# Gate and up products of an expert in one branch or in two, by halves of the weights' rows

## The chip, the cores and the metric

The kernel runs on one core of a Trainium2 chip. The metric is the device time of one execution in microseconds, and the figure for a kernel is the median of its runs. Three runs of the kernel before took 1243.87, 1243.13 and 1238.35 us: the median is 1243.13 us, the mean 1241.78 us.

## The reference

The block has two halves. The first mixes tokens: a diagonal state-space mixer and a stick-breaking attention share an input projection and an output projection. The change does not touch it. The second is a routed mixture of experts over 1024 tokens of width 1024. Each token goes to two of 32 experts, and of each expert is computed

```python
def expert_block(args):
    xb, e = args
    return (jax.nn.silu(xb @ w_gate[e]) * (xb @ w_up[e])) @ w_down[e]
```

`w_gate` and `w_up` are 1024 by 512, `w_down` is 512 by 1024, all float32. So an expert has 6 MB of weights, and 32 of them 192 MB. The result is scaled by the gate and added to the token's row.

## The kernel before, in words

**Stages.** In the profiled execution the projections, the mixer and the attention take the span up to some 584 us, the routing that up to some 600 us, and the loop over the experts the rest. All times below are from the span's start.

**Weights.** SyncE streams the weights as units of 1 MB in one fixed order (`load_units`, the issue is line 855). An expert has four units for the gate and up products, `hv[0]` to `hv[3]`: gate rows of the first half, up rows of the first half, gate and up rows of the second half. Two more units are for the down product. The units go into a ring of 17 tiles (named `rg`, `q_t`, `yT` and `rw` after what the memory held before), and the issue of a unit waits on SyncE until TensorE has done the last read of the tile's former content.

**Order of the experts.** Experts are sorted by count, and large and small ones alternate. For 18 of the 32 places in this order `two(e)` (line 1246) holds: such an expert may have more than 128 tokens, so that the code for a second block of up to 128 tokens is compiled for it. The places are 0, 1, 2, 4, 6, 8, 10, 12, 14, 16, 17, 18, 20, 22, 24, 26, 28 and 30. Blocks past the second are left to a loop at the end.

**Branches.** All counts are only known at run time, and every engine reads them into a register (`prep_n`, line 1283, for TensorE). `by_count` (lines 1361 to 1369) chooses among three forms: "all" over 64 tokens (32 matmuls of 128 by 512, line 1204), "half" over 32 (line 1210) and "quarter" (line 1216). `past` (lines 1371 to 1379) holds two nested Ifs: over 128 tokens (line 1375), and in it over 192 (line 1376). Where an If on TensorE is not taken, the other side has an instruction that puts the semaphore count where the taken side would have left it, and this instruction waits until all matmuls before it have ended. I call this a drain.

**One turn of the loop** for place e has on TensorE: the gate and up products of e (`in_`, line 1420), the transposes of the gathered rows of e+1 (`prep_x`, line 1381, at line 1194), the down products of e-1 (`down_`, lines 1222, 1228 and 1234), the index products of a later expert (`prep_p`, line 1295) and the transposes of e's hidden rows (`h_`, line 1463, at line 1240). GpSimd gathers rows (line 1184) and scatters results (line 1189). VectorE writes the one-hot matrices that `prep_p` multiplies: `OHa` for the first 128 tokens (two buffers), and `OHb` for the second block (one buffer, `OH2`, cleared by GpSimd at line 920).

**What the diff touches.** In `in_` the first block's products stand with `past` for the second block in one `by_count` (`in_many`), which is the whole of `in_` for every place but 0. Place 0 has its products in two `by_count` with the first index products (`between`) in the middle.

By the branches that left instructions in the profiled execution, the 18 places fall into three classes. Places 4, 8, 16 and 24 have a second block. Places 10, 12, 18, 20, 26 and 28 take "all" and have none. The other eight (0, 1, 2, 6, 14, 17, 22 and 30) take "half".

Of the kernel before, what the change touches and what calls it, by code (L numbers as in the profile page):

```python
# [10 lines left out]
BF = mybir.dt.bfloat16  # L11
# [9 lines left out]
NT = 8  # L21
P = 128
# [14 lines left out]
def block_kernel(ctx, tc, x, g_mix, w_in, lam_re, lam_im, log_dt, b_re, b_im, c_re, c_im, d_skip,  # L37
                 w_glu, b_glu, g_q, g_k, g_so, g_ao, w_out, g_ffn, w_rg, b_rg, w_re, b_rexp,
                 w_gate, w_up, w_down, out, dbg=None, stop=99):
    nc = tc.nc  # L40
# [717 lines left out]
    kp = ctx.enter_context(tc.tile_pool(name="kp", bufs=1, side="right", reuse_waits="tile"))  # L758
# [138 lines left out]
    slot2 = kp.tile([P, P], BF, name="slot2")  # L897
    ts(slot2, slot, float(P), None, op0=OP.add)

    slot2m = kp.tile([P, P], BF, name="slot2m")  # L900
# [15 lines left out]
    ts(sideq, sideq, 32.0, None, op0=OP.is_ge)  # L916
    tt(sided, side, sideq, op=OP.subtract)

    OH2 = kp.tile([P, NT, P], BF, name="OHb")
    nc.gpsimd.memset(OH2, 0.0)  # L920
    memb = late.tile([P, NT, NE], BF, name="memb")
    gts = late.tile([P, NT, NE], F32, name="gts")
    x2s = {}
# [202 lines left out]
    posb = kp.tile([P, NT, NE], BF, name="posb")  # L1126
# [27 lines left out]
    def one_hot(t_, pe, sl):  # L1154
        shp = [P, NT, P]
        tt(t_, sl.unsqueeze(1).to_broadcast(shp), pe.to_broadcast(shp), op=OP.is_equal)

    def ohs():
        return kp.tile([P, NT, P], BF, name="OHa", bufs=2)
# [19 lines left out]
    def pb(tag, bufs=2):  # L1179
        return ps.tile([P, 512], F32, tag=tag, bufs=bufs, name=tag)  # L1180
# [20 lines left out]
    def in_all(p, xt, hv, ks=range(8)):  # L1201
        for k_ in ks:
            for j in range(2):
                mm(p[j], xt[:, k_], hv[2 * (k_ // 4) + j][:, 512 * (k_ % 4):512 * (k_ % 4) + 512],  # L1204
                   start=k_ == 0, stop=k_ == 7)

    def in_half(pg, xt, hv, ks=range(8)):
        for k_ in ks:
            for r, j in ((LO, 0), (HI, 1)):
                mm(pg[r], xt[:, k_, LO], hv[2 * (k_ // 4) + j][:, 512 * (k_ % 4):512 * (k_ % 4) + 512],  # L1210
                   start=k_ == 0, stop=k_ == 7)

    def in_quarter(pg, xt, hv, ks=range(4)):
        for k_ in ks:
            for u in range(4):
                mm(pg[32 * u:32 * u + 32], xt[:, 4 * (u // 2) + k_, QU], hv[u][:, 512 * k_:512 * k_ + 512],
                   start=k_ == 0, stop=k_ == 3)
# [24 lines left out]
    def two(e):  # L1242

        if e < NF:
            return True
        b = int(f"{e:05b}"[::-1], 2)
        return (b - 1 - (b > 16) - (b > 8) + 1) * (P + 1) <= 2 * T

    def prep(e):

        if e >= NE:
            return
        d = EX.setdefault(e, {})
        ev = slice(e, e + 1)
        if e >= NF:
            ev = bass.ds(nc.values_load(evi[0:1, e:e + 1], engines=[ET.DVE], min_val=0, max_val=NE - 1), 1)
        sl = kp.tile([P, P], BF, name="sl")
        stt(sl, mid, some[:, e:e + 1], slotq, op0=OP.mult, op1=OP.add)
        stt(sl, top, many[:, e:e + 1], sl, op0=OP.mult, op1=OP.add)
        d["oh"] = ohs()  # L1260
        one_hot(d["oh"], posb[:, :, ev], sl)
        d["ax"] = aux[:, :, ev, :]
        if e >= NF:
            d["ax"] = kp.tile([P, NT, 1, 5], BF, name="ax", bufs=2)
            nc.vector.tensor_copy(d["ax"], aux[:, :, ev, :])
        d["ce"] = csi[0:1, e:e + 1]
        d["ng"] = nc.values_load(d["ce"], engines=[ET.Pool], min_val=0, max_val=T + HP)
        d["nv"] = nc.values_load(d["ce"], engines=[ET.DVE], min_val=0, max_val=T + HP)
        if not two(e):
            return  # L1270
        with tc.If(d["nv"] > P):
            with tc.If(d["nv"] <= P + HP) as few:
                one_hot(OH2, posb[:, :, ev], slot2m)
            with few.Else():
                one_hot(OH2, posb[:, :, ev], slot2)

    def prep_n(e):

# [8 lines left out]
    def prep_p(e):  # L1287

        if e >= NE:
            return  # L1290
        d = EX[e]
        d["pi"] = pb("y")[:, 0:16].rearrange("p (b n) -> p b n", b=2)
        for b_, oh in enumerate((d["oh"], OH2)[:2 if two(e) else 1]):
            for i in range(NT):
                mm(d["pi"][:, b_, 0:5], oh[:, i], d["ax"][:, i, 0], start=i == 0, stop=i == NT - 1)

# [64 lines left out]
    def by_count(n, all_, half, quarter):  # L1361

        with tc.If(n > HP) as many_:
            all_()
        with many_.Else():
            with tc.If(n > HP // 2) as some_:
                half()
            with some_.Else():
                quarter()

    def past(e, n, all_, half):

        if not two(e):
            return
        with tc.If(n > P):  # L1375
            with tc.If(n > P + HP) as many_:
                all_()
            with many_.Else():
                half()
# [36 lines left out]
    def next_raws(n):  # L1416
        raw_k[0] += n
        return [raws.pop(raw_k[0] - n + j) for j in range(n)]

    def in_(e, between=None):  # L1420

        d = EX[e]
        pg, pu = pb("acc"), pb("acc")
        pg2, pu2 = (pb("gx"), pb("gx")) if two(e) else (None, None)
        hv = next_raws(4)

        def in_many():
            in_all((pg, pu), d["xt"], hv)
            past(e, d["nt"], lambda: in_all((pg2, pu2), d["xt2"], hv), lambda: in_half(pg2, d["xt2"], hv))

        if e:
            by_count(d["nt"], in_many, lambda: in_half(pg, d["xt"], hv), lambda: in_quarter(pg, d["xt"], hv))
        else:
            for a in range(2):
                by_count(d["nt"], lambda: in_all((pg, pu), d["xt"], hv, range(4 * a, 4 * a + 4)),
                         lambda: in_half(pg, d["xt"], hv, range(4 * a, 4 * a + 4)),
                         lambda: in_quarter(pg, d["xt"], hv, range(2 * a, 2 * a + 2)))
                if a == 0:
                    between()
            d["turn2"]()  # L1440
            d["second"]()
            past(e, d["nt"], lambda: in_all((pg2, pu2), d["xt2"], hv), lambda: in_half(pg2, d["xt2"], hv))
        d["p"] = pg, pu, pg2, pu2

    def in_out(e):
# [126 lines left out]
    d = EX[0]  # L1572
# [8 lines left out]
    mo = ctx.enter_context(tc.tile_pool(name="mo", bufs=1, side="right", reuse_waits="tile"))  # L1581
    xga = [mo.tile([P, D], F32, name=f"xga{j}") for j in range(3)]
    xgb = mo.tile([P, D], F32, name="xgb")
    d["xg"] = xga[0]
    gather(xga[0], idx0, AL)
    for t_ in (xga[1], xga[2], xgb):
        nc.gpsimd.memset(t_, 0.0)
    tt(away, away, cnt.unsqueeze(1).to_broadcast(sh), op=OP.mult)
    tt(posb, own, away, op=OP.add)
# [4 lines left out]
    mo2 = ctx.enter_context(tc.tile_pool(name="mo2", bufs=1, side="right", reuse_waits="tile"))  # L1594
    prep_x(0)
    prep(0)
    prep_n(0)
    prep(1)
# [54 lines left out]
    with tc.For_i(0, nx, 1) as j:  # L1653
        ev = nc.values_load(xei[0:1, bass.ds(j, 1)], min_val=0, max_val=NE - 1)
# [20 lines left out]
        xt = mo.tile([P, 8, P], F32, name="xt2")  # L1675
# [9 lines left out]
        pg, pu = pb("acc"), pb("acc")  # L1685
# [39 lines left out]
```

## Time and profile before

| what | value |
|---|---|
| runs | 1243.87, 1243.13, 1238.35 us |
| profiled execution | 1238.39 us, of it span 1236.6 us |
| mean granted TensorE clock | 0.961 of full speed |
| TensorE busy (PE) | 1083.4 us, 88% |
| VectorE busy (DVE) | 632.3 us, 51% |
| ScalarE busy (ACT) | 342.9 us, 28% |
| GpSimd busy (POOL) | 261.7 us, 21% |
| moved by DMA | 267.87 MB, of it 232.29 MB on SyncE's queue |

PE is the matmul side of TensorE, PEld its weight loads; a name with a q behind it (PEq, PEldq, SPq) is an engine's sequencer, which reads the instructions and does the branches. The profiled execution is 1.8 us longer than its span, and 4.74 us (0.38%) shorter than the median of the runs.

### The profile page before, as it was taken

The numbers are of one execution on the slowest core, as the hardware profiler recorded it, in microseconds if no ns is written. First come the engines' busy times: TensorE is split into PE (matmuls) and PEld (weight loads), VectorE is DVE, ScalarE is ACT, GpSimd is POOL, SyncE is SP. The second block draws the span as 40 slices with busy tenths as digits, with TensorE's granted clock in tenths as the row PEclk, the third lists the DMA queues.
The fourth block names the chain that finished last, engine by engine and source line by source line (L and its number), as shares of the span: only waits on it lengthen the run. The fifth ranks groups of instructions, "written<-read, shape, count | busy, mean of one in ns | idle before, by whom it ended". The sixth has DMA issues, their size and how long they took to land. (4 is left out here: it accounts for less than half of the span.)

```text
span 1236.6 us, 19598 instructions
## 1 busy us (share of the span) xinstructions
PE 1083.4 (88%) x6562; PEld 698.4 (56%) x6562; DVE 632.3 (51%) x1487; ACT 342.9 (28%) x656; POOL 261.7 (21%) x401
## 2 busy tenths in 40 slices
PE   5999999978999879998586897998899988999985
PEld 5999899976776647887232333444334433434432
DVE  6888777779788865666722323213241422321211
ACT  6225244366668564322100000001010010100011
POOL 4043122033334410222111112002020020211111
PEclk9999999998999999999697998999999999999998
DMA  7251322120001135436699599679999899999993
GB/s 252 86 105 38 56 68 67 35 85 18 2 1 24 52 130 194 147 125 239 252 380 370 197 364 371 234 277 352 387 382 397 316 309 377 366 406 382 358 392 71
DMA packets 95577, 267.87 MB, mean 217 GB/s; under 512 B 44308, under 2 KB 57432, under 8 KB 70840
## 3 DMA queue, kind: packets, MB, share of 16 engines
q1 hardware_dynamic: 80664, 232.29, 50.6%
q0 software_dynamic: 11232, 27.04, 8.8%
q10 hardware_dynamic: 3520, 6.46, 1.4%
q8 instruction: 93, 1.52, 0.5%
q14 instruction: 68, 0.56, 0.1%
HBM read 240.73 MB, written 23.86 MB: 214 GB/s over the span
## 5 line engine op out<-in xcount | busy, mean ns | idle before, releaser
L91 PE MATMUL acc<-wh,hTh 128*128 128x256 f32 x512 | 147.0, 287 | 4.4 <-ACT wh L87 4.4
L92 PE MATMUL acc<-wl,hTh 128*128 128x256 f32 x512 | 145.8, 285 | 0.0
L93 PE MATMUL acc<-wh,hTl 128*128 128x256 f32 x512 | 144.9, 283 | 0.0
L91 PEld LDWEIGHTS acc<-wh,hTh 128*128 128x128 f32 x512 | 97.5, 191 | 5.0 <-ACT wh L87 5.0
L1189 POOL DMA_INDIRECT out_dram<-ysa,idx x24 | 36.8, 1533 | 299.6 <-DVE idx L1304 112.8
L92 PEld LDWEIGHTS acc<-wl,hTh 128*128 128x128 f32 x512 | 97.6, 191 | 0.7 <-DVE wl L88 0.6
L93 PEld LDWEIGHTS acc<-wh,hTl 128*128 128x128 f32 x512 | 97.4, 190 | 0.0
L697 DVE TENSOR_TENSOR_SCAN bb<-bb,sb 128x128 f32<-128x128 f32 (+7 forms) x64 | 90.0, 1420 | 14.0 <-POOL bb L694 13.5
L694 POOL TENSOR_SCALAR bb<-sb 128x128 f32<-128x128 f32 (+7 forms) x64 | 64.7, 1015 | 96.1 <-ACT sb L693 84.3
L1457 DVE TENSOR_TENSOR hs<-hs,acc 128x512 f32<-128x512 f32 x10 | 6.9, 688 | 146.4 <-ACT hs L1453 83.6
L1194 PE MATMUL tr<-ident,xga 128*128 128x128 f32 x256 | 39.8, 303 | 34.7 <-DMA xga<-h2d,idx 26.9
L1194 PEld LDWEIGHTS tr<-ident,xga 128*128 128x128 f32 x256 | 33.3, 195 | 60.4 <-issue 34.8
L1204 PE MATMUL acc<-rw,xt 128*128 128x512 f32 x128 | 56.9, 592 | 0.0
L1189 POOL DMA_INDIRECT out_dram<-ysf,idx x12 | 18.9, 1574 | 175.7 <-ACTq L1375 77.4
L708 PE MATMUL tr<-ident,bb 128*128 128x128 f32 x288 | 45.8, 283 | 8.8 <-DVE aT L714 3.6
L1452 ACT ACTIVATE hs<-acc 128x512 f32<-128x512 f32 x10 | 6.0, 598 | 170.0 <-PEq L1375 78.4
L91 PE MATMUL acc<-wh,mh 128*128 128x512 f32 x128 | 52.2, 410 | 0.0
L721 PE MATMUL acc<-aT,v_t 128*64 128x128 f32 x576 | 46.2, 281 | 5.8 <-DVE aT L714 4.8
L93 PE MATMUL acc<-wh,ml 128*128 128x512 f32 x128 | 50.8, 397 | 0.0
L92 PE MATMUL acc<-wl,mh 128*128 128x512 f32 x128 | 50.6, 396 | 0.0
L1184 POOL DMA_INDIRECT xga<-h2d,idx x32 | 35.0, 1095 | 68.1 <-PE y L1234 19.2
L1210 PE MATMUL acc<-rw,xt 128*64 128x512 f32 x192 | 46.8, 603 | 1.8 <-issue 1.8
(510 smaller groups left out, 2334.8 us busy)
## 6 DMA issues: line engine op xcount, KB each, us to landing
rw<-in_w_down_dram SPq DMA_DIRECT2D x28, 1024.0 KB
rw<-in_w_gate_dram SPq DMA_DIRECT2D x28, 1024.0 KB
rw<-in_w_up_dram SPq DMA_DIRECT2D x27, 1024.0 KB
rg<-in_w_gate_dram SPq DMA_DIRECT2D x20, 1024.0 KB
rg<-in_w_up_dram SPq DMA_DIRECT2D x20, 1024.0 KB
rg<-in_w_down_dram SPq DMA_DIRECT2D x20, 1024.0 KB
wraw<-in_w_in_dram SPq DMA_DIRECT2D x16, 512.0 KB
yT<-in_w_up_dram SPq DMA_DIRECT2D x8, 1024.0 KB
```

Of the source, the lines that this page charges most:

```text
L91: mm(o, ah, bh, start=first, stop=False)
L92: mm(o, ah, bl, start=False, stop=False)
L93: mm(o, al, bh, start=False, stop=last)
L694: nc.gpsimd.tensor_scalar(bt[:, off:T], st[:, off:T], -1.0, 1.0, op0=OP.mult, op1=OP.add)
L697: nc.vector.tensor_tensor_scan(rv, rv, sv, 0.0, op0=OP.mult, op1=OP.add)
L708: nc.tensor.transpose(pt[:, j * P:(j + 1) * P], st[:, off + (j0 + j) * P:off + (j0 + j + 1) * P], ident)
L721: mm(po[64 * r:64 * r + 64, :P], v_t[:, j, 64 * h:64 * h + 64], ATT["T", h, i][:, j, :], start=j == 0, stop=j == i)
L1184: nc.gpsimd.indirect_dma_start(out=dst[r], out_offset=None, in_=h2d, in_offset=bass.IndirectOffsetOnAxis(ap=idx[:n, :1], axis=0))
L1189: nc.gpsimd.indirect_dma_start(out=rows, out_offset=bass.IndirectOffsetOnAxis(ap=idx[:n, :1], axis=0), in_=src[r], in_offset=None, compute ...
L1194: nc.tensor.transpose(pt[:, c], xg[:, 4 * cg + c::8], ident)
L1204: mm(p[j], xt[:, k_], hv[2 * (k_ // 4) + j][:, 512 * (k_ % 4):512 * (k_ % 4) + 512], start=k_ == 0, stop=k_ == 7)
L1210: mm(pg[r], xt[:, k_, LO], hv[2 * (k_ // 4) + j][:, 512 * (k_ % 4):512 * (k_ % 4) + 512], start=k_ == 0, stop=k_ == 7)
```

## The change

`in_` of a place with `two(e)` is written as two `by_count`, one after the other: the first with rows 0 to 3 of the first half of the weights (`hv[0]`, `hv[1]`), the second with rows 4 to 7 (`hv[2]`, `hv[3]`). Each has its own `past`, so the order of the products is first block, second block by the first half of the weights, then first block, second block by the second half. The other 14 places keep one `by_count`, and place 0 keeps its form. `OHb` becomes two tiles, used by e modulo 2, which live in the pool `mo` and are cleared after the first gather and not at line 920.

```diff
--- before.py
+++ after.py
@@ -916,8 +916,6 @@
     ts(sideq, sideq, 32.0, None, op0=OP.is_ge)
     tt(sided, side, sideq, op=OP.subtract)
 
-    OH2 = kp.tile([P, NT, P], BF, name="OHb")
-    nc.gpsimd.memset(OH2, 0.0)
     memb = late.tile([P, NT, NE], BF, name="memb")
     gts = late.tile([P, NT, NE], F32, name="gts")
     x2s = {}
@@ -1270,9 +1268,9 @@
             return
         with tc.If(d["nv"] > P):
             with tc.If(d["nv"] <= P + HP) as few:
-                one_hot(OH2, posb[:, :, ev], slot2m)
+                one_hot(OH2[e % 2], posb[:, :, ev], slot2m)
             with few.Else():
-                one_hot(OH2, posb[:, :, ev], slot2)
+                one_hot(OH2[e % 2], posb[:, :, ev], slot2)
 
     def prep_n(e):
 
@@ -1290,7 +1288,7 @@
             return
         d = EX[e]
         d["pi"] = pb("y")[:, 0:16].rearrange("p (b n) -> p b n", b=2)
-        for b_, oh in enumerate((d["oh"], OH2)[:2 if two(e) else 1]):
+        for b_, oh in enumerate((d["oh"], OH2[e % 2])[:2 if two(e) else 1]):
             for i in range(NT):
                 mm(d["pi"][:, b_, 0:5], oh[:, i], d["ax"][:, i, 0], start=i == 0, stop=i == NT - 1)
 
@@ -1424,22 +1422,28 @@
         pg2, pu2 = (pb("gx"), pb("gx")) if two(e) else (None, None)
         hv = next_raws(4)
 
-        def in_many():
-            in_all((pg, pu), d["xt"], hv)
-            past(e, d["nt"], lambda: in_all((pg2, pu2), d["xt2"], hv), lambda: in_half(pg2, d["xt2"], hv))
-
-        if e:
-            by_count(d["nt"], in_many, lambda: in_half(pg, d["xt"], hv), lambda: in_quarter(pg, d["xt"], hv))
-        else:
-            for a in range(2):
-                by_count(d["nt"], lambda: in_all((pg, pu), d["xt"], hv, range(4 * a, 4 * a + 4)),
-                         lambda: in_half(pg, d["xt"], hv, range(4 * a, 4 * a + 4)),
-                         lambda: in_quarter(pg, d["xt"], hv, range(2 * a, 2 * a + 2)))
-                if a == 0:
-                    between()
+
+        for a in range(2):
+            k8, k4 = range(4 * a, 4 * a + 4), range(2 * a, 2 * a + 2)
+
+            def in_many():
+                in_all((pg, pu), d["xt"], hv, k8)
+                if e:
+                    past(e, d["nt"], lambda: in_all((pg2, pu2), d["xt2"], hv, k8),
+                         lambda: in_half(pg2, d["xt2"], hv, k8))
+
+            if e == 0 or two(e):
+                by_count(d["nt"], in_many, lambda: in_half(pg, d["xt"], hv, k8),
+                         lambda: in_quarter(pg, d["xt"], hv, k4))
+            if e == 0 and a == 0:
+                between()
+        if e == 0:
             d["turn2"]()
             d["second"]()
             past(e, d["nt"], lambda: in_all((pg2, pu2), d["xt2"], hv), lambda: in_half(pg2, d["xt2"], hv))
+        elif not two(e):
+            by_count(d["nt"], lambda: in_all((pg, pu), d["xt"], hv), lambda: in_half(pg, d["xt"], hv),
+                     lambda: in_quarter(pg, d["xt"], hv))
         d["p"] = pg, pu, pg2, pu2
 
     def in_out(e):
@@ -1581,9 +1585,10 @@
     mo = ctx.enter_context(tc.tile_pool(name="mo", bufs=1, side="right", reuse_waits="tile"))
     xga = [mo.tile([P, D], F32, name=f"xga{j}") for j in range(3)]
     xgb = mo.tile([P, D], F32, name="xgb")
+    OH2 = [mo.tile([P, NT, P], BF, name=f"OHb{j}") for j in range(2)]
     d["xg"] = xga[0]
     gather(xga[0], idx0, AL)
-    for t_ in (xga[1], xga[2], xgb):
+    for t_ in OH2 + [xga[1], xga[2], xgb]:
         nc.gpsimd.memset(t_, 0.0)
     tt(away, away, cnt.unsqueeze(1).to_broadcast(sh), op=OP.mult)
     tt(posb, own, away, op=OP.add)
```

The rows below are the compiled order on an engine, without times; a name in brackets is a semaphore that the instruction waits for. First TensorE before, at place 4 (its weights lie in `q_t` and `yT`): from the If of line 1375 behind the first block's products to the not-taken side of it.

```order
L1375 COMPARE_AND_BRANCH
L1376 COMPARE_AND_BRANCH
L1204 MATMUL gx<-q_t,xt_8073 128x512 [waits PE_49,Activation_49]
L1204 MATMUL gx<-q_t,xt_8073 128x512 [waits DVE_49]
L1204 MATMUL gx<-q_t,xt_8073 128x512 x6
L1204 MATMUL gx<-yT,xt_8073 128x512 x8
L1376 UNCONDITIONAL_BRANCH
L1210 MATMUL gx<-q_t,xt_8073 64x512 [waits PE_49,Activation_49]
L1210 MATMUL gx<-q_t,xt_8073 64x512 x7
L1210 MATMUL gx<-yT,xt_8073 64x512 x8
L1376 UNCONDITIONAL_BRANCH
L1375 UNCONDITIONAL_BRANCH [waits PE_49]
```

The two lines with 64x512 belong to a second block of at most 64 tokens. The last row is the drain: it waits for PE itself, once, behind all 32 products of the first block.

TensorE after, same place, the end of the first half (line 1202 is line 1204 of before, 1373 is 1375, 1374 is 1376):

```order
L1202 MATMUL acc<-q_t,xt 128x512 x6
L1373 COMPARE_AND_BRANCH
L1374 COMPARE_AND_BRANCH
L1202 MATMUL gx<-q_t,xt_8083 128x512 [waits PE_49,Activation_49]
L1202 MATMUL gx<-q_t,xt_8083 128x512 [waits DVE_49]
L1202 MATMUL gx<-q_t,xt_8083 128x512 x6
L1374 UNCONDITIONAL_BRANCH
L1208 MATMUL gx<-q_t,xt_8083 64x512 [waits PE_49,Activation_49]
L1208 MATMUL gx<-q_t,xt_8083 64x512 x7
L1374 UNCONDITIONAL_BRANCH
L1373 UNCONDITIONAL_BRANCH [waits PE_49]
```

The drain now stands behind the 16 products with `q_t`. What follows it on the way of a place without second block is the jump over the other forms to the second `by_count`:

```order
L1361 UNCONDITIONAL_BRANCH
L1373 UNCONDITIONAL_BRANCH
L1326 UNCONDITIONAL_BRANCH
L1361 UNCONDITIONAL_BRANCH
L1490 UNCONDITIONAL_BRANCH
L1492 UNCONDITIONAL_BRANCH
L1361 COMPARE_AND_BRANCH
L1202 MATMUL acc<-yT,xt 128x512 [waits DMAHW1_49]
L1202 MATMUL acc<-yT,xt 128x512 [waits DMAHW2_49]
L1202 MATMUL acc<-yT,xt 128x512 x6
L1373 COMPARE_AND_BRANCH
```

So the products with `yT` begin behind a compare of their own, and behind them comes the same If of line 1373 with the same drain: it stands twice on the way of an expert that takes "all" and has no second block. Of the "quarter" form each half reads all four weight tiles (`in_quarter` picks two of its four rows), so that the last reader of all four tiles is in the second `by_count`, and the counts that SyncE's issues wait for stand at the same ends as before. TensorE's program grows from 7824 to 7989 rows.

GpSimd before, from the first gather to the first count it reads:

```order
L1184 DMA xga_6748<-h2d,idx_6736 128x1024 [waits DMAHW4_49,DMAHW3_49,DMAHW5_49,DMAHW2_49,DMAHW6_49,DMAHW1_49,DMAHW7_49,DMAHW0_49,DVE_49]
L1587 MEMSET xga_6749 128x1024 [waits PE_49]
L1587 MEMSET xga_6750 128x1024 [waits PE_49,Activation_49]
L1587 MEMSET xgb 128x1024 [waits PE_49]
L1267 TENSOR_LOAD csi [waits DVE_49]
```

And after:

```order
L1182 DMA xga_6746<-h2d,idx_6734 128x1024 [waits DMAHW4_49,DMAHW3_49,DMAHW5_49,DMAHW2_49,DMAHW6_49,DMAHW1_49,DMAHW7_49,DMAHW0_49,DVE_49]
L1592 MEMSET OHb_6750 128x1024 [waits PE_49,Activation_49]
L1592 MEMSET OHb_6751 128x1024
L1592 MEMSET xga_6747 128x1024
L1592 MEMSET xga_6748 128x1024 [waits Activation_49]
L1592 MEMSET xgb 128x1024
L1265 TENSOR_LOAD csi [waits DVE_49]
```

Two memsets of 128 by 1024 bf16 have moved in between the first gather and the count of place 0; they stood as one at line 920.

## Rows read from the trace of the kernel before

**Rows 1.** Busy time by stretch: length, engines (instructions), clock, DMA share, GB/s.

```profile
600.00:700.00 100.00, 77.85 (x380) 32.97 (x377) 32.38 (x80) 7.05 (x15) 12.50 (x9) 0.86 0.84 312
700.00:840.00 140.00, 123.30 (x536) 55.21 (x537) 38.25 (x95) 11.91 (x26) 20.82 (x16) 0.94 0.86 309
840.00:915.00 75.00, 65.00 (x352) 28.07 (x352) 25.28 (x65) 7.44 (x16) 15.05 (x11) 0.95 1.02 389
915.00:1221.00 306.00, 279.09 (x1280) 123.54 (x1272) 85.60 (x221) 29.54 (x63) 44.38 (x35) 1.00 0.96 355
```

**Rows 2.** TensorE's waits, 600 to 1236 us: total, times, longest.

```profile
PE tr L1194 <- DMA xga<-h2d,idx: 21.8, 4, 9.1
...
PE tr L1194 <- issue: 7.8, 6, 1.4
...
PE gx L1194 <- DMA xgb<-h2d,idx: 3.1, 2, 1.9
...
PE y L1222 <- DMA yT<-in_w_gate_dram: 0.4, 1, 0.4
```

**Rows 3.** SyncE's issues, 745 to 842 us: start, length.

```profile
763.04 0.33 SPq L855 DMA_DIRECT2D rw<-in_w_up_dram  x1
...
837.54 0.33 SPq L855 DMA_DIRECT2D yT<-in_w_down_dram  x1
```

**Rows 4.** TensorE at place 10: start, length, [idle before, releaser].

```profile
823.52 7.03 PE L1204 MATMUL acc<-yT,xt 128*128 128x512 f32 x16
830.39 7.03 PE L1204 MATMUL acc<-rw,xt 128*128 128x512 f32 x16
838.68 1.16 PE L1194 MATMUL tr<-ident,xga 128*128 128x128 f32 x8 [1.26 <-issue]
```

**Rows 5.** TensorE at places 28 to 30.

```profile
1179.54 1.14 PE L1194 MATMUL tr<-ident,xga 128*128 128x128 f32 x8 [1.41 <-issue]
...
1199.10 0.72 PE L1240 MATMUL tr<-ident,hs 128*128 128x128 f32 x4 [0.53 <-PEq L1375]
```

**Rows 6.** TensorE at the start of place 18.

```profile
980.88 1.12 PE L1204 MATMUL acc<-rg,xt 128*128 128x512 f32 x2 [0.31 <-PEq L1473]
```

**Rows 7.** Matmuls of line 1204: duration min/median/max in ns.

```profile
L1204 PE MATMUL acc<-rw,xt x128: 592/592/595, 764.8 to 1177.5; 128*128 128x512 f32 x128
```

**Rows 8.** Branches of line 1375, TensorE's sequencer: duration min/median/max in ns.

```profile
L1375 PEldq COMPARE_BRANCH  x33: 65/208/490, 610.1 to 1198.8; - x33
```

**Rows 9.** The same for line 1366.

```profile
L1366 PEldq COMPARE_BRANCH  x70: 70/180/3247, 599.1 to 1216.3; - x70
```

**Rows 10.** TensorE waits for gathered rows of place 8.

```profile
757.57 1.94 PE L1194 MATMUL gx<-ident,xgb 128*128 128x128 f32 x8 [1.87 <-DMA xgb<-h2d,idx]
```

**Rows 11.** TensorE's products of place 8.

```profile
764.77 13.90 PE L1204 MATMUL acc<-rw,xt 128*128 128x512 f32 x32
778.50 13.90 PE L1204 MATMUL gx<-rw,xt 128*128 128x512 f32 x32
792.24 1.05 PE L1194 MATMUL tr<-ident,xga 128*128 128x128 f32 x8
```

**Rows 12.** TensorE at place 22, which takes "half".

```profile
1056.88 7.09 PE L1210 MATMUL acc<-rw,xt 128*64 128x512 f32 x32
1063.90 1.15 PE L1194 MATMUL tr<-ident,xga 128*128 128x128 f32 x8
```

**Rows 13.** GpSimd at the start of the loop.

```profile
594.38 1.86 POOL L1587 MEMSET xga<- 128x1024 f32 x2
...
607.43 0.95 POOL L1184 DMA_INDIRECT xga<-h2d,idx  x1 [10.30 <-DVE sl L1258]
```

**Rows 14.** TensorE's first read of `OHb`.

```profile
605.60 0.34 PE L1295 MATMUL y<-aux,OHb 128*128 128x5 bf16 x8
```

**Rows 15.** TensorE at place 2.

```profile
636.79 3.65 PE L1210 MATMUL acc<-rw,xt 128*64 128x512 f32 x16 [1.82 <-issue]
```

**Rows 16.** A stretch at half clock.

```profile
880.50:883.80 3.30, 2.63 (x16) 0.66 (x20) 1.66 (x4) 0.37 (x1) 2.09 (x2) 0.50 1.01 420
```

## The prediction

> **What bounds the kernel now.** I read first the busy time by stretch over the loop of experts [rows 1]. After 700 us TensorE works in 87 to 91% of every stretch; before that in 78%. The weights' stream is nearly as full: the DMA share is 0.84 to 1.02. Two resources so close to full mean that the busy shares alone don't tell which of them ends last, so the next view is TensorE's list of waits [rows 2]. The only wait there for a weight is one of 0.4 us. The long ones are the gathered rows (21.8 us in four waits, and 3.1 us in two for second blocks), and then many of about 1 us for branches, semaphores and VectorE. So TensorE's own chain of products and turnarounds bounds the loop, and not the weights. SyncE's issues agree [rows 3]: the last unit of place 10 is issued at 763.04, and TensorE reads it only from 830.39 on [rows 4]; the issue at 837.54 stands right behind the end of place 10's products at 837.42, which is the ring being full and SyncE waiting for TensorE. What the change does must therefore be read on TensorE, at the ends and the middles of `in_`.
>
> **What an `in_` costs now.** At place 10, "all" without second block, the products with the first half of the weights take 823.52 to 830.55, those with the second half 830.39 to 837.42, without a gap; then TensorE is idle for 1.26 us until the transposes at 838.68 [rows 4]. There are six such idle times, 7.8 us in sum and 1.4 us the longest [rows 2, 5], one for each of the six places of that kind. That is the drain of the If of line 1375: the sequencer waits for the last matmul, jumps, loads the next count and only then gives out work. Where a second block is there, as at place 8, the 64 products and the transposes follow each other without a gap [rows 11]. Where "half" is taken, as at place 22, too [rows 12].
>
> **The added drain.** At each of the six places the same If now stands behind the first 16 products as well, so TensorE runs dry between 830.39 and the following product, six times in the loop.
> - The idle time of one. The nearest row is the drain of the same If in `down_` at 1199.10, without a load of a count behind it: 0.53 us [rows 5]. Behind the new drain comes one more compare, of `by_count`, before the first product; the compares of line 1375 have a median of 208 ns [rows 8]. I take 0.53 + 0.21 = 0.74 us.
> - The lost overlap. A matmul takes 0.592 us from start to end [rows 7], but 16 of them take 7.03 us, so they start (7.03 - 0.59)/15 = 0.429 us apart. An idle time counts from the end of the last, so another 0.592 - 0.429 = 0.16 us is lost.
> - Sum: 0.90 us at each place, 6 x 0.90 = 5.4 us. Nothing lies beside it: the next product needs the same queue, and `down_`, the transposes and the index products all stand behind on it.
> - Bounds: the cheapest drain in the rows is 0.31 us, an If not taken before a compare and a product [rows 6], which gives 6 x (0.31 + 0.16) = 2.8 us. The dearest is the longest of `in_`, 1.41 us with the load of the count that the new one lacks [rows 5]: 6 x 1.57 = 9.4 us. I keep 0 as a floor, for the case that the wait is absorbed (below). A gain from the drain itself is excluded, since the second drain of `in_` stays as it was.
> - What can't absorb it: the waits for gathered rows, of which the last in the trace is over at 757.57 us [rows 10]. The six places come after it, at 830 and later.
>
> **The parts that I cost at nothing.**
> - "Half" places, seven of them newly split. They leave by a jump, not by a drain. At place 22 the last product ends at 1063.97 and the transposes start at 1063.90, though the sequencer jumped and loaded the next count between them [rows 12]: it ran ahead of the array by more than that takes. A second jump in the middle is hidden by the same lead. If that cover were gone, each would cost about the 0.74 us from above, 7 x 0.74 = 5.2 us.
> - Places with a second block, four of them. The way is the taken side, without a drain, and at place 8 the step from the first block's products to the second's has no gap [rows 11]; the change makes three such steps of one. `xt2`, which is wanted some 7 us sooner, is written by VectorE long before. The last first-block product ends 7 us later than now, but ScalarE and VectorE need its sums only behind the transposes and the down products of the place before. If the cover is gone: three compares of 0.21 us at four places, 2.5 us.
> - The weights. As SyncE's waits stand at the same ends as before, no unit is issued earlier; behind each new drain all units that wait for this place are issued 0.9 us later, which the long lead of a unit [rows 3, 4] covers. Cost and gain 0; were TensorE to wait for them, no more than the drains' 5.4 us again.
> - The two memsets. One of the single `OHb` took place in an idle time of GpSimd before; two of them, each as long as half of the 1.86 us that two float32 memsets of the same number of elements take, stand now between the first gather and the others [rows 13]: 1.9 us later. Behind them GpSimd is idle for 10.30 us before the gather at 607.43, which waits for VectorE. The first read of `OHb` on TensorE comes at 605.60 [rows 14], 9 us after both would be done. Cost 0; without that idle time 1.9 us. The second `OHb` could spare VectorE a wait for its readers only at places 1 and 17, and there TensorE has no wait for it in the list: gain 0.
>
> **The sum.** 1238.39 us, the profiled execution, plus 5.4 us is 1243.8 us. This execution is as fast as the fastest run and 0.38% under the median of 1243.13 us; two of three runs are slower by 5 us, and nothing tells which the next ones will be. I set the sum on the mean of the three runs, 1241.8 us: **1247.2 us**, 0.3% above the median. With the bounds of the drain, 1244.6 to 1251.2 us. About 0.5% (6.2 us) is what a measurement of this kernel can tell from no change; so faster means under 1236.9 us and slower over 1249.3 us.
>
> **Rivals.**
> 1. *The drain is absorbed.* From 915 to 1221 us the DMA share is 0.96 [rows 1]; if there the weights set the pace, TensorE would lose in a drain what it would otherwise wait for. Then the time is 1241.8 us, or with half absorbed 1244.5. Against it: 0.4 us of waits for weights in the whole loop [rows 2]. Chance 0.19.
> 2. *Faster.* Halves let weight tiles go sooner, the stream closes up earlier, and the gathers, which share the DMA engines with it, land sooner. The place is the four and two waits for gathered rows, 24.9 us [rows 2]. Should half of that go, 12.4 us less and 5.4 more: 1234.8 us; it decides if the sooner release shortens these waits by over 5.4 us. For it: the DMA share is 0.84 to 0.86 where these waits lie, so the stream has idle time to close up. Against it: the counts that SyncE waits for stand at the same ends. Chance 0.11.
> 3. *Slow jumps.* The branches of line 1366 have a median of 180 ns but a longest of 3247 ns [rows 9], and at place 2 TensorE was idle for 1.82 us before its products [rows 15]. The change adds a branch in 17 places, with targets past the other forms. If three of them hit TensorE with 2.5 us each, the time is 1247.2 + 7.5 = 1254.7 us; from one such jump on it is slower by over 0.5%. Against it: of more than a hundred such branches only a few are long, and those behind "half" are hidden by the lead. [...] Chance 0.10.
> 4. *The clock.* Six more idle times could make TensorE's granted clock fall. [...] Against it: from 915 to 1221 us the clock is 1.00 although four drains of 1.3 to 1.4 us lie there [rows 1, 5]. [...] Chance 0.10.
>
> **How the numbers follow.** The forecast has the remaining 0.50, of which 0.11 lies above 1249.3 us (dear drains, or runs like the slower two). Slower: 0.11 + 0.10 + 0.10 = 0.31. Faster: rival 2, 0.11. Within 0.5%: 0.39 + 0.19 = 0.58. The range for 8 in 10 goes down to 1238 us, where a fast execution with absorbed drains lies, and up to 1256 us, between the prices of rivals 3 and 4; it leaves out most of rival 2 and part of rival 4.
>
> **What would show it.** Right: at places 10, 12, 18, 20, 26 and 28 an idle time of 0.5 to 1.0 us between the two runs of 16 products, with the If of line 1373 named as releaser, beside the old ones of 1.3 to 1.4 us before the transposes; no gap in the middle of places 8 and 22; SyncE's issues at the same ends; the loop 4 to 7 us longer. Wrong: waits for gathered rows well under 21.8 us, or TensorE waiting for weights; a clock under 1.00 after 915 us; single idle times of 2 us or more at the new branches; or no idle time in the middle of the six places at all.

## The result, and the profile after

The changed kernel takes 1255.7 us (median of four runs, 1254.8 to 1257.2), the kernel before 1242.33 us in the same comparison. The ratio is 1.0114, 95% interval 1.0087 to 1.0141: the change costs some 13 us, where I had forecast 5 us and called no measurable change the likeliest. The profiled execution took 1257.2 us with a span of 1255.5 us, 18.9 us more than the span of before, whose profiled execution was a quick one of its kernel.

The same stretches as in [rows 1], columns as there:

```profile
600.00:700.00 100.00, 74.69 (x371) 31.98 (x371) 33.22 (x81) 6.87 (x14) 12.64 (x9) 0.83 0.86 315
700.00:840.00 140.00, 123.45 (x538) 54.81 (x535) 37.23 (x92) 11.61 (x25) 19.98 (x16) 0.93 0.84 304
840.00:915.00 75.00, 63.68 (x316) 26.81 (x314) 22.19 (x57) 7.64 (x16) 12.62 (x9) 0.98 1.02 377
915.00:1221.00 306.00, 275.80 (x1220) 120.74 (x1222) 85.89 (x223) 26.82 (x57) 44.14 (x35) 0.97 0.96 356
```

The clock of the long stretch is 0.97, where it was 1.00. TensorE's waits, the list that answers to [rows 2] (line numbers are two or four away from before: 1192 is 1194, 1202 is 1204, 1208 is 1210, 1361 is 1363, 1373 is 1375):

```profile
PE tr L1192 <- DMA xga<-h2d,idx: 27.2, 4, 9.0
...
PE tr L1192 <- issue: 7.0, 6, 1.3
...
PE acc L1202 <- PEq L1373: 4.0, 6, 0.8
PE acc L1208 <- issue: 3.7, 3, 1.6
PE gx L1192 <- DMA xgb<-h2d,idx: 2.7, 2, 1.8
```

Two larger entries are new in the loop's later part: 4.0 us in six waits before line 1202, and 3.7 us in three before line 1208. (A single wait of 0.9 us before the index products at 931.45 us is new there too. Before the first drain stand 5.4 us more of waits for gathered rows, and one wait of 1.9 us for a weight at 632.01 us. The gathered rows' waits alone range from 20.6 to 26.2 us over the traces of the kernel before and of its copies with unused code below, so their rise is not put down to the change.) The first is the added drain, here at place 10 ([rows 4] before; start, length, then in brackets the idle time before and its releaser):

```profile
826.60 7.03 PE L1202 MATMUL acc<-yT,xt 128*128 128x512 f32 x16
834.17 7.13 PE L1202 MATMUL acc<-rw,xt 128*128 128x512 f32 x16 [0.55 <-PEq L1373]
842.63 1.14 PE L1192 MATMUL tr<-ident,xga 128*128 128x128 f32 x8 [1.32 <-issue]
```

The second stands in the middle of the half form at places 14, 22 and 30. Place 14 and, in the next fence, place 22:

```profile
901.95 3.65 PE L1208 MATMUL acc<-rw,xt 128*64 128x512 f32 x16
906.75 0.62 PE L1208 MATMUL acc<-rw,xt 128*64 128x512 f32 x1 [1.14 <-issue]
```

```profile
1069.23 3.65 PE L1208 MATMUL acc<-rw,xt 128*64 128x512 f32 x16
1073.90 1.51 PE L1208 MATMUL acc<-rw,xt 128*64 128x512 f32 x6 [1.02 <-issue]
```

At place 30 it is 1.59 us. A row of 16 products covers 3.65 us, then TensorE waits for its sequencer, which stands in a branch. The branches of line 1361, the compare of `by_count` (duration min/median/max in ns; before, as line 1363, its longest was 1332, and the longest of line 1366 was 3247 [rows 9]):

```profile
L1361 PEldq COMPARE_BRANCH  x82: 65/208/4687, 599.5 to 1236.5; - x82
```

The long ones begin at 902.21 (4.20 us), 1069.49 (4.07 us) and 1218.69 (4.69 us), and each ends 0.3 us before the products go on. What the DMA queues did from 902.2 to 906.5 us (packets, bytes, share of the engines):

```profile
q1 hardware_dynamic: 233, 1.71, 96.2%
...
q8 instruction: 1, 0.02, 1.5%
```

One packet of the instruction queue falls into it, 16 KB, at 903.9 to 905.0 us. From 30 to 566 us, before the loop, one such packet comes for every 255 instructions of TensorE, in the mean of 30 and in both kernels. So I read it as the sequencer waiting for the next piece of TensorE's program, beside a weight stream that takes 96% of the engines. One such meeting could be chance, since some sixty of these packets fall into the loop. But TensorE has 58 branches of over 2 us in the loop, counted from 598 us on over the traces of both kernels and of all runs below, and each of them ends 1.3 to 1.65 us after the end of a 16 KB packet of this queue (1.35 to 1.53 us for the eight of the two kernels). So these branches wait for code.

The places with a second block run on without a gap, as before [rows 11]; here is place 8:

```profile
769.55 7.03 PE L1202 MATMUL acc<-rw,xt 128*128 128x512 f32 x16
776.42 7.03 PE L1202 MATMUL gx<-rw,xt 128*128 128x512 f32 x16
783.29 7.03 PE L1202 MATMUL acc<-rw,xt 128*128 128x512 f32 x16
790.16 7.03 PE L1202 MATMUL gx<-rw,xt 128*128 128x512 f32 x16
797.02 1.04 PE L1192 MATMUL tr<-ident,xga 128*128 128x128 f32 x8
```

And the granted clock fell to half, 0.50, in three stretches after 1040 us, where the kernel before had 1.00 up to 1221 us [rows 1]:

```profile
1049.90:1053.30 3.40, 3.34 (x8) 1.04 (x10) 2.19 (x5) 0.00 (x0) 1.56 (x2) 0.50 1.01 422
1121.60:1125.00 3.40, 3.40 (x9) 0.97 (x10) 1.86 (x5) 0.40 (x2) 1.75 (x2) 0.50 1.02 422
1203.50:1206.90 3.40, 3.40 (x20) 1.53 (x16) 0.00 (x0) 0.00 (x0) 0.91 (x1) 0.50 1.00 405
```

They lie at places 21, 25 and 29. What TensorE did before the first, a short row of products, an idle time of 1.96 us and one of 0.68 us, stands in the profile of before too (1.96 and 0.81 us), and no half level follows there.

**Where the 18.9 us of span are.** Up to the start of place 10 the loop is 3.1 us later (826.60 against 823.52), and what follows the last products is 1.6 us shorter. Between the two points, 823.52 to 1221.18 before and 826.60 to 1241.72 after, the loop is 17.5 us longer. The six drains are 4.0 us of idle time and 6 x 0.16 = 1.0 us of lost overlap, less 0.8 us by which the six old ones became shorter (7.8 to 7.0): 4.2 us. The three idle times at places 14, 22 and 30 are 3.75 + 0.5 = 4.2 us. TensorE's busy time within half-clock stretches, halved, is what they lose: at place 21 the 16 products from 1049.96 us on, 3.34 us of them in such a stretch, take 5.30 us where a row at full clock takes 3.65. By this it is 9.8 us after, 3.1 before, 6.7 more. (The three stretches above make 5.1 of it; the rest is that two others, at 886.1 and 916.8 us, hold more busy time than those at 880.5 [rows 16] and 911.2 us before.) The rest, 2.4 us, is spread over small idle times. So three causes of like size, of which the forecast had the first.

### The profile page after: what moved, and what is told of

Its sections match the earlier page's. It is cut to its first block, busy times and chain, and to the rows that moved or that the text cites. A ratio compares the mean times of both kernels' runs of the same rounds, so it can differ in the third digit from the quotient of the medians.

```text
span 1255.5 us, 19678 instructions
## 1 busy us (share of the span) xinstructions
PE 1090.4 (87%) x6562; PEld 699.9 (56%) x6562; DVE 633.7 (50%) x1487; ACT 342.0 (27%) x656; POOL 261.1 (21%) x402
## 5 line engine op out<-in xcount | busy, mean ns | idle before, releaser
L1187 POOL DMA_INDIRECT out_dram<-ysf,idx x12 | 18.9, 1573 | 180.4 <-ACTq L1373 80.8
L1208 PE MATMUL acc<-rw,xt 128*64 128x512 f32 x192 | 50.6, 640 | 4.4 <-issue 3.7
```

The lines of the kernel that those rows point to most:

```text
L1187: nc.gpsimd.indirect_dma_start(out=rows, out_offset=bass.IndirectOffsetOnAxis(ap=idx[:n, :1], axis=0), in_=src[r], in_offset=None, compute ...
```

## The experiments

All were timed in five rounds against the kernel before. The ratio is to its runs, with the 95% interval.

| run | median us | ratio |
|---|---|---|
| e1_one_past | 1245.85 | 1.0022 (1.0001 to 1.0043) |
| e2_two_pasts | 1253.02 | 1.0072 (1.0044 to 1.0101) |
| e3_one_onehot | 1254.63 | 1.0085 (1.0063 to 1.0108) |
| e4_place10 | 1247.62 | 1.0020 (0.9995 to 1.0045) |
| p1_after_64 | 1241.63 | 0.9983 (0.9963 to 1.0003) |
| p2_after_126 | 1253.63 | 1.0081 (1.0060 to 1.0101) |
| p3_before_64 | 1252.72 | 1.0060 (1.0044 to 1.0077) |
| p4_before_126 | 1247.03 | 1.0027 (1.0006 to 1.0047) |
| q_after_32 | 1246.33 | 1.0024 (1.0006 to 1.0042) |
| q_after_96 | 1257.97 | 1.0101 (1.0078 to 1.0125) |
| q_before_32 | 1249.58 | 1.0047 (1.0028 to 1.0065) |
| q_before_96 | 1248.86 | 1.0043 (1.0022 to 1.0064) |
| r1_after_idle | 1247.00 | 1.0044 (1.0027 to 1.0062) |
| r2_after_code | 1242.76 | 1.0008 (0.9989 to 1.0027) |
| r3_before_idle | 1245.45 | 1.0025 (1.0004 to 1.0046) |
| r4_before_code | 1244.86 | 1.0019 (0.9995 to 1.0043) |

**The parts, e1 to e4.** e1 takes the first of the two drains out of the changed kernel: the second block's products, of both halves, stand behind the second half of the first block's; e2 puts it into the kernel before, without a second `by_count`; e3 goes back to one tile `OHb`, cleared where it was; e4 is e2 at place 10 alone.

```diff
# e1, on the changed kernel
-                if e:
-                    past(e, d["nt"], lambda: in_all((pg2, pu2), d["xt2"], hv, k8), ...
+                if e and a == 1:
+                    past(e, d["nt"], lambda: in_all((pg2, pu2), d["xt2"], hv), ...
# e2, on the kernel before (e4: only where e == 10)
-            in_all((pg, pu), d["xt"], hv)
-            past(e, d["nt"], lambda: in_all((pg2, pu2), d["xt2"], hv), ...
+            for a in range(2):
+                k8 = range(4 * a, 4 * a + 4)
+                in_all((pg, pu), d["xt"], hv, k8)
+                past(e, d["nt"], lambda: in_all((pg2, pu2), d["xt2"], hv, k8), ...
```

> The two branches by halves stay, but the second block stands once, behind the second half's products, so the drain of its If stands once per place as before. Theory A (sum of parts: drains 0.9 us at six places, slow jumps of 1.0 to 1.6 us exposed at places 14, 22 and 30, the rest half-clock stretches that follow from them): the six idle times in the middle go, the three at 14, 22 and 30 stay: 1255.7 - 5.4 = about 1250 us. Rival B (the clock alone: half-clock stretches come from the drains, jumps matter little): 1242 to 1245 us, clock about 0.961. Rival C (any small delay shifts the work against the clock's grid and costs some 7 us whatever it is): still 1253 to 1256 us.

> One by_count per place as before, but inside its all-form the second block's If stands twice, by halves: the added drains without the added branch for half and quarter. Theory A: six idle times of 0.5 to 0.8 us in the middle, none at places 14, 22 and 30: 1242.3 + 5.4 = about 1248 us, more if half-clock stretches follow. Rival B (clock from drains): the full 1255 us. Rival C: 1249 to 1255 us.

> The change without its second part: OHb is one tile again and is cleared where it was. Theory A: nothing from this part, 1255.7 us within 2 us. Rival D (the later memsets and the other places in memory cost the 0.8 us that the first transposes of the loop come later, and shift the rest): 1250 us or less.

> The kernel before with the second block's If twice at place 10 alone: one added drain. Theory A: 1242.3 + 0.9 = 1243.2 us, clock as before (0.961). Rival C (a shift of under 1 us changes which stretches fall to the half clock): 3 to 7 us more or less than before, with half-clock stretches after 915 us that the kernel before has not.

e3 agrees with the forecast: the tiles and the moved memsets bring nothing that can be told from the changed kernel. e1 has no gap in the middle of place 10:

```profile
824.57 7.03 PE L1202 MATMUL acc<-yT,xt 128*128 128x512 f32 x16
831.44 7.03 PE L1202 MATMUL acc<-rw,xt 128*128 128x512 f32 x16
```

But of the three idle times only that at place 14 is left, and it is longer:

```profile
904.60 0.61 PE L1208 MATMUL acc<-rw,xt 128*64 128x512 f32 x1 [1.87 <-issue]
```

In e2 the drain alone leaves 829.38 - (822.20 + 7.03) = 0.15 us of idle time, where no jump over other forms and no compare of `by_count` come behind it in the code:

```profile
822.20 7.03 PE L1204 MATMUL acc<-yT,xt 128*128 128x512 f32 x16
829.38 7.11 PE L1204 MATMUL acc<-rw,xt 128*128 128x512 f32 x16
```

That is 6 x (0.15 + 0.16) = 1.9 us in all, and still the kernel is some 9 us slower (ratio 1.0072). The largest single piece of it lies where it has no branch at all, inside the 32 products of the half form at place 14:

```profile
894.59 1.93 PE L1210 MATMUL acc<-rw,xt 128*64 128x512 f32 x6
899.81 5.39 PE L1210 MATMUL acc<-rw,xt 128*64 128x512 f32 x12 [3.29 <-issue]
```

A packet of the instruction queue falls into this gap as well (897.34 to 898.40 us), and the products go on 1.4 us after it. So e1 and e2 can't be read as the price of the drain with and without the second branch: each edit moved all code behind it, and the idle times moved with the code. Nor do their times fit the sums of theory A well: e1 lies 4 us under 1250 us, e2 5 us over 1248 us. e4 ended between the two expectations with a wide spread, 1239.6 to 1251.3 us, and does not tell the two theories apart. This led to the next runs.

**The place of the code, p1 to p4 and the q runs.** Matmuls that are never run, put into an If before place 0 that is not taken:

```diff
     prep_n(0)
+    dead = [pb("acc"), pb("acc")][0]
+    with tc.If(EX[0]["nt"] > P + HP):
+        for i in range(64):
+            mm(dead[:, 0:2], oh0[:, i % NT], aux[:, i % NT, 0, TOK], start=True, stop=True)
     prep(1)
```

Each is two rows of TensorE's program. The number in a run's name is that of the matmuls; 126 of them with the If are the 256 rows that the expectations take for one 16 KB piece; the packets before the loop gave 255 instructions to one.

> The changed kernel with 64 small matmuls (128 rows of TensorE's program) that are never run, behind an If that place 0 does not take, while TensorE waits for the first gathers. Nothing that is run in the loop differs, only where its code lies against the 16 KB pieces in which the trace shows TensorE's program being loaded. Theory A' (drains 5 us, the exposed loads of code at places 14, 22 and 30 and the half-clock stretches behind them the rest): the stalls of 1 to 3 us move to other places or vanish; the time moves by 2 us or more, to 1248 to 1262 us, while the six idle times in the middle of `in_` stay at 0.5 to 0.8 us. Rival E (the second branch itself is slow at these places, wherever the code lies): same places, same 1255 us within 1.5 us.

> The same with 126 matmuls that are never run, with their loads and the If about 256 rows, which is one 16 KB piece. Theory A': the code in the loop lies against the pieces nearly as without them, so stalls are nearly at the same places and the time is 1255 us within 2 us. Rival E: the same, so this run tells only with the one before: both equal speaks for E, the first different and this one not for A'.

> The kernel before with the 64 matmuls that are never run. Theory A': the loads of code that were hidden at places 14, 18 and 22 move, and some come into the open: 1241 to 1250 us, not equal to before by more than 2 us, with idle times of 1 to 3 us at other places than now. Rival E: as before, 1243 us within 1.5 us.

> The kernel before with 126 matmuls that are never run, about one piece: by A' and by E as before, 1243 us within 2 us, with the longest idle time at place 2 as now.

p1 is 14 us quicker than the changed kernel and not slower than the one before, with the six drains still there (0.55 to 0.66 us; place 10, then place 14 in the next fence):

```profile
826.98 7.03 PE L1202 MATMUL acc<-yT,xt 128*128 128x512 f32 x16
834.67 7.12 PE L1202 MATMUL acc<-rw,xt 128*128 128x512 f32 x16 [0.66 <-PEq L1373]
```

```profile
900.12 4.08 PE L1208 MATMUL acc<-rw,xt 128*64 128x512 f32 x17
903.61 0.59 PE L1208 MATMUL acc<-rg,xt 128*64 128x512 f32 x1
```

At place 14 the 17th product follows the 16th within one row, without idle time, and none stands at 22 and 30. One load came into the open elsewhere, in the middle of place 2:

```profile
645.23 3.65 PE L1208 MATMUL acc<-rw,xt 128*64 128x512 f32 x16 [2.21 <-issue]
```

There TensorE next waits for gathered rows, for 2.13 us where the changed kernel waited 4.41 us, so that this idle time is made up. p1's time is under the 1248 to 1262 us that theory A' gave: the place of the code was worth more than the theory had. p2, shifted by one whole piece, has them back at 14, 22 and 30 with 1.07, 0.99 and 1.71 us (its profiled execution, 1263.82 us, was the slowest of its six):

```profile
907.30 3.65 PE L1208 MATMUL acc<-rw,xt 128*64 128x512 f32 x16
912.03 0.61 PE L1208 MATMUL acc<-rw,xt 128*64 128x512 f32 x1 [1.07 <-issue]
```

The kernel before, shifted by half a piece (p3), is with 1252.7 us beyond the 1250 us expected at most. It gets 4.79 us of idle time before place 22, with its products partly at half clock behind it, and the branch that TensorE waits for, of line 1363, has 5552 ns where the longest was 1332:

```profile
1061.53 0.72 PE L1240 MATMUL tr<-ident,hs 128*128 128x128 f32 x4
1067.05 10.03 PE L1210 MATMUL acc<-rw,xt 128*64 128x512 f32 x32 [4.79 <-issue]
```

```profile
L1363 PEldq COMPARE_BRANCH  x65: 65/208/5552, 601.1 to 1231.3; - x65
```

Shifted by a whole piece (p4) it has its own pattern back, the three long branches of line 1366 (2.60, 2.98 and 2.72 us, where they were 2.62, 3.25 and 2.65) as well as the 1.82 us at place 2 [rows 15]:

```profile
642.85 7.09 PE L1210 MATMUL acc<-rw,xt 128*64 128x512 f32 x32 [1.83 <-issue]
```

That both patterns come back after 256 rows bears out this length of a piece. So rival E falls: it is the place of the code against the 16 KB pieces that decides where the second branch waits, not the branch as such. p4's time is not that of before within the 2 us expected, and its jump over the unused code itself takes 5.9 us at the start of the loop. In p2 this jump takes 6.9 us, so that p2's nearness to the changed kernel's time is in part chance: taken against p4, which has the same jump, p2 is 6.6 us slower and not 13.

> The changed kernel with 32 matmuls that are never run (64 rows, a quarter of a 16 KB piece). If the place of the code decides (theory A'), its time lies anywhere from 1241 to 1258 us, and its idle times over 1 us in the loop lie at other places than 14, 22 and 30 or have another length there; the six drains stay at 0.5 to 0.8 us. Averaged over shifts of 0, 64, 128 and 192 rows the change should cost its drains, some 5 us, over the kernel before averaged in the same way. Rival F (the change is nearly free, and its 13 us are all the place of the code): that average within 2 us of none.

> The same with 96 matmuls that are never run (192 rows). Theory A': 1241 to 1258 us, with the average over the four shifts 5 us over that of the kernel before; rival F: average within 2 us.

> The kernel before with 32 matmuls that are never run. Theory A': 1238 to 1254 us, decided by which loads of code come into the open; an idle time of over 1 us stands at each place where TensorE's sequencer shows a branch of over 2.5 us without work queued before it.

> The kernel before with 96 matmuls that are never run. Theory A': 1238 to 1254 us, by the same rule. Should one of the eight kernels of the two rows be clear of the kernel before on the fast side, it is the version that beats both.

q_after_32 has none of the three idle times, q_after_96 has 1.68 and 1.75 us at places 14 and 22, q_before_32 has 3.8 us at place 14, and it stands inside a row of products, as in e2, where no long branch is: the rule in its expectation does not find it. q_before_96 has 3.6 us at the start of the loop and two of 1.1 and 1.3 us later. Over shifts of 0, 64, 128 and 192 rows the changed kernel's mean ratio is 1.0056 and that of before 1.0038: the change itself comes to 0.18%, 2.2 us. By the scatter over four shifts each, the standard error of that is 4 to 5 us, so it decides neither for the 5 us of theory A' nor for rival F. Taken in pairs of equal shift (0, 64, 128, 192 and 256 rows) the change costs 13.4, -3.3, -11.1, 9.1 and 6.6 us between the medians: its sign depends on the place of the code. None of the shifted kernels beats the kernel before beyond its interval.

**Idle time and clock, r1 to r4.** r1 and r3 have two Ifs, not taken, in the middle of the half form at places 14, 22 and 30 of p1 and of the kernel before; in the controls r2 and r4 the same code is in the quarter form, which is not run there. The edit of r1:

```diff
+        def idle(n=2):
+            if e not in (14, 22, 30):
+                return
+            for _ in range(n):
+                with tc.If(d["nt"] > P + HP):
+                    mm(pg2, d["xt"][:, 0], hv[0][:, 0:512], start=True, stop=True)
...
-                by_count(d["nt"], in_many, lambda: in_half(pg, d["xt"], hv, k8),
+                by_count(d["nt"], in_many, lambda: (in_half(pg, d["xt"], hv, k8), a == 0 and idle()),
```

> The changed kernel with the 64 matmuls that are never run (1241.6 us, no stall at places 14, 22 and 30), and in the middle of these three places, on the way of `half`, two Ifs that are not taken: three idle times of about 1 us. Theory G (idle times there cost themselves and the half-clock stretches that follow): over its control, which has the same Ifs where they are never run, by 8 us or more, with half-clock stretches behind places 14, 21, 25 or 29. Rival H (the stretches come by themselves): over its control by the idle times alone, 3 to 4 us.

> Control of the run before: the same two Ifs in the form `quarter` of places 14, 22 and 30, which no expert there takes. By both theories 1241.6 us, unless the few added rows of code move a load into the open.

> The kernel before with the same two Ifs in the middle of `half` at places 14, 22 and 30. Theory G: 8 us or more over its control; rival H: 3 to 4 us over it.

> Control of the run before: the Ifs in the form `quarter`. By both theories 1243 us, unless the added rows move a load of code into the open.

The idle times came, at place 14 1.36 us in r1 and 0.58 us in r3:

```profile
892.10 3.65 PE L1208 MATMUL acc<-rw,xt 128*64 128x512 f32 x16
897.11 0.61 PE L1208 MATMUL acc<-rw,xt 128*64 128x512 f32 x1 [1.36 <-PEq L1429]
```

```profile
900.51 3.65 PE L1210 MATMUL acc<-rw,xt 128*64 128x512 f32 x16
904.75 0.61 PE L1210 MATMUL acc<-rw,xt 128*64 128x512 f32 x1 [0.58 <-PEq L1431]
```

r1 has 4.7 us of them in sum (2.0 at place 22), its control one of 1.9 us at place 22, a load of code. So 2.8 us more of idle time, 3.1 with the lost overlap of two, make 4.2 us more time; in r3 three of 0.58 to 0.72 us, 2.4 us with the overlap, make 0.6 us more. By the scatter of the runs the two differences are uncertain by 1.7 and 2.9 us (95%). That is nearer to rival H: idle times of up to 2 us at these places cost about themselves. Theory G, by which they draw half-clock stretches behind them and cost 8 us or more, falls. For longer ones nothing is shown; the 4.79 us of p3 do have a half-clock stretch behind them.

**The clock by itself.** In 109 runs the kernel before took 1235.2 to 1254.4 us, mean 1242.7. Its runs with a lower mean granted clock are longer, 9.1 us for each 0.01; its mean clock is 0.956, that of the changed kernel's four runs 0.955. The profiled execution of before, at 0.961, was 4.3 us under that mean. So of the 6.7 us that the pair of profiles shows for the clock, most is that execution's luck. The clock goes with the place of the code to some degree: the mean over the runs is 0.959 in p1 and 0.949 in p3, which at 9.1 us for each 0.01 are 2 us less and 6 us more than at 0.956. What decides whether a stretch such as that at place 21 falls I could not settle: the same work is at full clock in one trace and at half in another, and p2, e3 and q_after_96 have their falls at the very places of the changed kernel (21, 25 and 29). Among the nine traced kernels with two `by_count` at a place, the six with an idle time in the middle of place 14 all fall at place 21, and the three without (p1, q_after_32, r2) do not; among those with one, e4, q_before_96 and r4 fall there without such an idle time, and e2 does not fall with one. So a link is neither shown nor excluded, and r1 against r2 bounds what it could cost at some 3 us.

## Why the prediction was wrong

- *The added drain* was right: 0.55 to 0.77 us of idle time where 0.74 was worked out, 5.0 us with the overlap where 5.4 was; the old ones became 0.8 us shorter in return. Only here did the forecast look for a cost. It stands at the six places named, with the old ones of 1.1 to 1.3 us beside it.
- *"'Half' places ... A second jump in the middle is hidden by the same lead"* is the step that failed. The lead at the end of 32 products had been enough for a branch of 2.65 us at place 22 (from 1059.53 us); in the middle it is one row of 16, 3.65 us, and the branches there took 4.1 to 4.7 us as they met a piece of code not yet loaded. Cost 4.2 us instead of 0. I had priced the loss of that cover by an ordinary drain, 0.74 us a place. The longest branch in [rows 9], 3.25 us, would not have warned me either, for it is shorter than the row of 3.65 us: the waits of 4.1 to 4.7 us appear only with the new place of the code.
- *Rival 3, slow jumps*, was this mechanism, at three places as I had put it, and its price of 7.5 us was a little nearer to the 4.2 us than my 0. That its total, 1254.7 us, lies so near to the measured 1255.7 us is luck, since the rest of that comes from the clock and from times not assigned. Its chance of 0.10 was too low, because I counted how rare the long branches are and not what the change does to them: it moves all code of the loop, so the few that were hidden by luck [rows 9] are dealt anew. p1 to p4 show it: with the place of the code alone the changed kernel's time moves by 14 us (p1), as much as the whole 13 us that the change seemed to cost. The long branch at place 14 took 4.20 us, with a packet of 16 KB in it.
- *Rival 4, the clock*, came about in part and not as told: half-clock stretches appeared after 915 us, but at places 21, 25 and 29 and not behind the drains, and r1 to r4 don't show that idle times bring them. The range ends at 1256 us, below a price of this rival with a half-clock stretch behind each new drain. No run shows that term; the trace of the changed kernel shows the three stretches, and 6.7 us more lost at half clock in the loop than before. Of the signs named for being wrong this one came true, a clock of 0.97 after 915 us.
- *Places with a second block, the weights, the memsets, `OHb`* were right at nothing: no gap at place 8, and e3 like the changed kernel. The one wait for a weight, 1.9 us, comes before the first new drain, and q_before_32 and r4, without the change, have such waits too (1.5 and 0.9 us). The issue behind place 10's products still stands at their end, 841.42 us against 841.30:

```profile
841.42 0.33 SPq L855 DMA_DIRECT2D yT<-in_w_down_dram  x1
```

- *The base.* I set the sum on the mean of three runs, 1241.8 us; 109 runs have 1242.7, so that wasn't the fault. Nor do drains, exposed loads and clock explain all of the miss: of the 13.4 us between the medians drains and exposed loads account for 8.4, the mean clock for about 1; some 4 us are not assigned to a cause.

## What to carry to other kernels

In a program with many run-time branches an edit is measured together with the new place of all code behind it, which alone moved the changed kernel from 1241.6 to 1258.0 us here: shift the kernel before and the kernel after by parts of a piece with code that is never run, before a difference of 1% is put down to the edit; a shift by a whole piece is the control. A jump was free here as long as the work queued ahead of it outlasted the branch itself, not the median branch of 0.18 to 0.21 us: at place 22, 2.65 us stayed hidden behind 7.09 us of products before, and 4.07 us behind 3.65 us left TensorE idle for 1.02 us after. And the longest branch in one trace is no bound, as 3.25 us before became 4.69 us after. Last, a profile is one draw: look at the clock's scatter over the runs before two profiles are subtracted.

## What I had not expected of the hardware

Unused code in front of the loop moved the time of the same work from 1241.6 to 1258.0 us (after) and from 1243.0 to 1252.7 us (before). A branch within the loop's turns that had to wait for a 16 KB piece took up to 5.55 us (p3) beside a weight stream that took 98% of the engines, and its packet itself 1.1 us (1064.24 to 1065.30 us). Whatever a long branch's length, its end came 1.3 to 1.65 us after its packet's. And products without any branch between them can wait as well, 3.29 us within one row in e2.
